# Layer 1's attention with the values as PE's weights: two query tiles move at once, and the root of the mean square is taken on summed columns

## The chip, the core and the metric

The kernel runs on one core of one Trainium2 chip. Time is device time in microseconds (us) from one launch to its end. The engines are PE (matmuls, with weight loads counted apart as PEld), DVE (vector), ACT (activation functions and copies), POOL (GpSimd) and SP, whose queue issues nearly all transfers.

## What is computed

A two-layer block over 512 latent tokens and 256 context tokens of width 1024. Layer 0 is grouped attention in two kinds, layer 1 differential attention; each is followed by a SwiGLU feed-forward. The change lies in layer 1's attention, which has 8 heads of two 64-wide halves:

```python
s = einsum('bqhad,bkhad->bhaqk', qb, k) * scale     # a: the two halves
p = softmax(s, axis=-1)
a = p[:, :, 0] - lam * p[:, :, 1]
o = einsum('bhqk,bkhe->bqhe', a, v)                 # e: 128 values a head
...
o = _rms(o, subln_w) * (1.0 - lam_init)             # over the 128 values of a head
out = o.reshape(n, heads * 128) @ w_out
x = x + gate * out
```

`_rms(x, w)` is x / sqrt(mean(x^2) + EPS) * w. Layer 1 is the last, so only the 512 latent tokens are queries; keys and values come from all 768.

## The kernel before

Tokens are cut into tiles of 128: t = 0..3 latent (NTX = 4), 4 and 5 context (NT = 6 in all). PE's instructions run in the order in which the program writes them; the other engines' and SP's are put in order by a planner that simulates the schedule. Each engine then works its list in order.

Layer 1's attention is a loop over i = 4 h + t (head h, query tile t), 32 steps. `attend1` is a generator with three parts, and the loop runs the parts of different steps beside each other, with two half tiles of the next head's input projection (`step()`, lines 466 to 468) between them:

- `scores(i)`: the two halves' scores on PE (L715, L716), the maximum on DVE (L718), the exponential with its row sum `sm` on ACT (L720), and the combination E0 + rt E1 on DVE (L723 to L727), where rt = -lam sm0 / sm1.
- `transposed(i)`: six PE transposes of the combined 128 x 768 tile (L734), copied to `PT` by ACT (four of them, L739) and DVE (two, L737), so that keys lie on partitions.
- `values(i)`: six fp32 matmuls (L744) with a 128 x 128 piece of `PT` as weights and a 128 x 128 piece of the values `vv` moving, summed in `av`. The output has queries on partitions. ACT scales it by 1 / sm0 (L746) and squares it with a sum along the row (L749); POOL takes (ss / 128 + EPS)^-0.5 (`rsqrt`, L159 and L160); DVE multiplies by root and `subln` (L751) into `o_t[t]`, a 128 x 1024 tile for each query tile.

The output projection needs heads and values on partitions. `OutProj.operand` transposes `o_t[t]` in groups of up to four 128 x 128 pieces on PE (L798), and ACT and DVE write the high part (L799) and the low part (L800) of the result. `term(t, n, k)` then is three matmuls of 512 columns (L807 to L809) for tile t, output half n and head k; `added` empties the bank by a DVE product with the gate (L473) and adds to the residual (L474).

The last six steps, i = 26 to 31 (`last` = 27), and the projection's terms beside them are written out by hand behind the loop, together with the loads and splits of the output weights (`wo1`, L759 and L762). There the order on PE is that of the calls. Two PSUM banks called acc0 and acc1 take the sums: acc0 the projections, acc1 `av` and half of the output sums; two further pairs of banks (`sc`) take scores, and tr0 and tr1 the transposes.

Of the kernel before, what the change touches and what calls it, by code (L numbers as in the profile page):

```python
# [19 lines left out]
P = 128  # L20
# [43 lines left out]
def backbone(es: ExitStack, tc: tile.TileContext, x, c, ctx, c_ctx, mod_w, mod_b, norm_mix_w, norm_ffn_w,  # L64
# [51 lines left out]
    def f32(ap):  # L116
        return ap.bitcast(F32)
# [38 lines left out]
    def rsqrt(ss, n, inv, tag):  # L156

        r = small.tile([P, n], F32, name="rs_" + tag, tag="rs_" + tag)
        nc.gpsimd.tensor_scalar(r, ss, inv, EPS, ALU.mult, ALU.add)  # L159
        nc.gpsimd.tensor_tensor(r, r, neghalf[:, :n], ALU.pow)  # L160
        return r
# [212 lines left out]
    def load_x(t, back=False):  # L374
        xt = keep.tile([P, D], F32, name=f"x{t}", tag="xo", bufs=6)
        src, t0 = (out if back else x, t) if t < NTX else (ctx, t - NTX)
        nc.sync.dma_start(xt, src[0, t0 * P:(t0 + 1) * P, :])
        return xt
# [324 lines left out]
                nc.scalar.copy(kT[:, :, t * P:(t + 1) * P], f32(pk))  # L703
            return transposes

    def attend1(h, t, state, o_t, nlam, subln, mp):
        qs, kT, vv = state.qs, state.kT, state.vv
        mx = small.tile([P, 2], F32, name="mx", tag="mx")
        sm = small.tile([P, 2], F32, name="sm", tag="sm")
        E = []  # L710
        for a in range(2):
            sc = p_sc.pool.tile([P, 1024], F32, name="sc", tag="sc", bufs=2)
            for s0, k0, k1 in ((256, SEQ, TOK), (512, 0, SEQ)):
                so = sc[:, s0:s0 + k1 - k0]
                nc.tensor.matmul(so, qs[t][:, 0, a, :], kT[:, a, k0:k1], start=True, stop=False)  # L715
                nc.tensor.matmul(so, qs[t][:, 1, a, :], kT[:, a, k0:k1], start=False, stop=True)  # L716
            s = sc[:, 256:256 + TOK]
            nc.vector.tensor_reduce(mx[:, a:a + 1], s, AX.X, ALU.max, negate=True)  # L718
# [3 lines left out]
        rc = small.tile([P, 2], F32, name="rc", tag="rc")  # L722
        nc.vector.reciprocal(rc, sm)  # L723

        rt = small.tile([P, 1], F32, name="rt", tag="rt")
        nc.vector.scalar_tensor_tensor(rt, sm[:, 0:1], nlam, rc[:, 1:2], ALU.mult, ALU.mult)
        nc.vector.scalar_tensor_tensor(E[0], E[1], rt, E[0], ALU.mult, ALU.add)  # L727
        yield
        vt = [4, 5, 0, 1, 2, 3]
        pts = []  # L730
        for g0, m in ((0, 4), (4, 2)):
            pt = tr_tile("ppt", [P, 4, P])
            for a in range(m):
                nc.tensor.transpose(pt[:, a, :], E[0][:, (g0 + a) * P:(g0 + a + 1) * P], ident)  # L734
            PT = mp.tile([P, 4, P], F32, name="PT", tag="PT", bufs=3)
            if g0:
                nc.vector.tensor_copy(PT[:, :m], pt[:, :m])  # L737
            else:
                nc.scalar.copy(PT, pt)  # L739
            pts += [PT[:, a, :] for a in range(m)]  # L740
        yield
        av = acc_tile("av", P, one=1)
        for kc, PT in enumerate(pts):
            nc.tensor.matmul(av, PT, vv[:, vt[kc], :], start=kc == 0, stop=kc == NT - 1)  # L744
        oc = o_t[t][:, h * P:(h + 1) * P]
        nc.scalar.activation(oc, av, AF.Copy, scale=rc[:, 0:1])  # L746
        ss = small.tile([P, 1], F32, name="oss", tag="oss")
        o1 = mp.tile([P, P], F32, name="o1", tag="o1", bufs=2)
        nc.scalar.activation(o1, oc, AF.Square, accum_out=ss)  # L749
        r = rsqrt(ss, 1, 1.0 / P, "o")  # L750
        nc.vector.scalar_tensor_tensor(oc, oc, r, subln, ALU.mult, ALU.mult)  # L751


    def out_load(k, raw):
        turn["load"] = nc.sync.dma_start(raw, od_w_out[0, k * P:(k + 1) * P, :])
# [22 lines left out]
    class OutProj:  # L778
# [5 lines left out]
            for i in range(2 if self.l == 0 else 1):  # L784
                self.g[i] = gate_row(self.l, 2, i, pool)

        def operand(self, t, parts=((0, 4), (4, 8)), bank=tr_tile):
            ohi, olo = tile_T(0, t), tile_T(1, t)
            if self.l == 0:
                if self.xs[t] is None:  # L790
                    self.xs[t] = load_x(t)
                nc.scalar.copy(ohi, self.o_t[t])
                nc.vector.tensor_sub(olo, self.o_t[t], f32(ohi))
                return
            for k0, k1 in parts:
                pt = bank("opt", [P, 4, P])
                for k in range(k0, k1):
                    nc.tensor.transpose(pt[:, k - k0, :], self.o_t[t][:, k * P:(k + 1) * P], ident)  # L798
                turn["opt"] = nc.scalar.copy(ohi[:, k0:k1], pt[:, :k1 - k0])  # L799
                nc.vector.tensor_sub(olo[:, k0:k1], pt[:, :k1 - k0], f32(ohi[:, k0:k1]))  # L800
            if k1 == KT:
                self.xs[t] = load_x(t, True)

        def term(self, t, n, k, ps):
            hi, lo = tile_T(0, t)[:, k, :], tile_T(1, t)[:, k, :]
# [760 lines left out]
    if True:  # L1566
# [28 lines left out]
                turned()  # L1595
        nlam = neg_lambda(lqk, cp)
        with behind("load"):
            subln = at.pool.tile([P, P], F32, name="subln")
            nc.sync.dma_start(subln, dram_rows(od_subln[0]))
# [3 lines left out]
        o_t = [keep.tile([P, D], F32, name=f"o{t}", tag="xo", bufs=6) for t in range(NTX)]  # L1603
        xs = xs1
        attend = {}

        def scores(i):
            h, t = divmod(i, NTX)
            attend[i] = attend1(h, t, state[h], o_t, nlam, subln, at.pool)
            next(attend[i])  # L1610

        def transposed(i):
            next(attend[i])

        def values(i):
            if i in attend:
                for _ in attend.pop(i):
                    pass

        last = 8 * NTX - 5  # L1620
        ws, raws = [], []
# [31 lines left out]

        def acc1(name, shape):
            return acc_tile(name, one=1).rearrange("p (k c) -> p k c", c=P)

        def part(*ks):
            if ks[0] == 0:
                part.ps = acc_tile("ops", one=0)
# [2 lines left out]
            if ks[-1] == KT - 1:  # L1662
                oproj.added(0, 0, part.ps, opa.pool, nc.gpsimd)

        def acc1(name, shape):
            return acc_tile(name, one=1).rearrange("p (k c) -> p k c", c=P)
# [52 lines left out]
        values(last + 3)  # L1719
        part(7)  # L1720
        for k in range(4, 6):
            oproj.term(0, 1, k, two[:, 0])
        oproj.operand(1)
        for k in range(6, KT):
# [4 lines left out]
        values(last + 4)  # L1729
        oproj.operand(2)  # L1730
        states[0].close()
        at.close()
# [155 lines left out]
```

## Time and profile before

| | us |
|---|---|
| median of 3 runs | 1695.99 (1693.12 to 1697.33) |
| the profiled execution | 1692.5 |
| its span, first to last instruction | 1690.7 |
| PE busy | 1628.1 (96%) |
| DVE / ACT / POOL busy | 1143.5 / 938.4 / 695.1 |

A row of the profile's groups gives line, engine, operation, the tiles (out<-in), the shape and the count; a row of the timeline gives start, duration, engine, line and shape, and in brackets the idle time before it with what ended it. Durations of matmuls overlap, since they are pipelined: what one costs is the distance from one start to the next.

### The profile page before, as it was taken

How to read it: one execution, taken by the hardware profiler on the slowest of the kernel's cores; microseconds unless marked ns; L12 is line 12 of the kernel's file. 1: busy time of each engine (PE TensorE's matmuls, PEld its weight loads, DVE VectorE, ACT ScalarE, POOL GpSimd, SP SyncE). 2: the span in 40 equal slices, each digit the busy share in tenths (PEclk: the TensorE clock that was granted, in tenths of full speed). 3: DMA queues.
4: the chain of work that ended last, by engine and by line, in shares of the span. 5: the costliest groups of instructions: out<-in, count | busy, mean ns of one | idle time of the engine just before them, and what ended most of it. 6: DMA issues, size and time to landing. Idle time of an engine off the chain costs nothing. (4 is left out here: it accounts for less than half of the span.)

```text
span 1690.7 us, 28553 instructions
## 1 busy us (share of the span) xinstructions
PE 1628.1 (96%) x10378; PEld 1465.3 (87%) x10378; DVE 1143.5 (68%) x2012; ACT 938.4 (56%) x2011; POOL 695.1 (41%) x867
## 2 busy tenths in 40 slices
PE   6999999899999999999999989999999999999998
PEld 3877777677999999998877889999988899999887
DVE  3765656754799887767767656666666598887433
ACT  5565555745456665544664456666666555555321
POOL 2665554321445554412413366666665242221000
PEclk9999999999999999999999999999999999999999
DMA  9222221411455555439966311111112433331431
GB/s 315 75 71 71 73 70 51 173 52 39 134 162 174 165 158 161 135 107 348 307 184 184 98 42 38 47 45 43 46 47 101 124 94 103 108 103 57 137 99 63
DMA packets 217964, 194.64 MB, mean 115 GB/s; under 512 B 20000, under 2 KB 202592, under 8 KB 217824
## 3 DMA queue, kind: packets, MB, share of 16 engines
q1 hardware_dynamic: 217472, 192.62, 36.9%
q8 instruction: 81, 1.33, 0.3%
q14 instruction: 59, 0.48, 0.1%
q10 hardware_dynamic: 352, 0.21, 0.0%
HBM read 179.92 MB, written 12.87 MB: 114 GB/s over the span
## 5 line engine op out<-in xcount | busy, mean ns | idle before, releaser
L901 ACT CAST wbh<-wr 128x512 fp32r<-128x512 f32 x170 | 104.9, 621 | 139.4 <-PE p L933 78.6
L933 PE MATMUL p<-hT,wbh 128*128 128x256 f32 (+1 forms) x752 | 154.4, 299 | 0.0
L911 POOL TENSOR_TENSOR wbl<-wr,wbh 128x512 fp32r<-128x512 f32 x43 | 60.2, 1400 | 174.2 <-ACT wbh L901 174.2
L933 PEld LDWEIGHTS p<-hT,wbh 128*128 128x128 f32 x752 | 121.9, 191 | 0.2
L911 DVE TENSOR_TENSOR wbl<-wr,wbh 128x512 fp32r<-128x512 f32 x127 | 106.4, 847 | 22.2 <-ACT wbh L901 17.8
L933 PE MATMUL p<-hT,wbl 128*128 128x256 f32 (+1 forms) x376 | 111.9, 298 | 0.0
L933 PE MATMUL p<-t,wbh 128*128 128x384 f32 (+1 forms) x480 | 111.3, 318 | 0.0
L604 POOL TENSOR_SCALAR Pt<-Pt,rc 128x256 f32<-128x256 f32 (+3 forms) x96 | 73.1, 772 | 86.9 <-DVE rc L601 79.6
L231 POOL TENSOR_TENSOR modp<-modp 128x512 f32<-128x512 f32 x40 | 57.3, 1433 | 116.5 <-ACT modp L230 116.5
L933 PE MATMUL p<-hTt,wbh 128*128 128x256 f32 (+1 forms) x480 | 101.0, 303 | 0.0
L466 PE MATMUL inps<-wih,hT 128*128 128x384 f32 x256 | 90.0, 351 | 7.2 <-ACT qkv L677 7.2
L887 POOL TENSOR_TENSOR wr<-wr 128x512 f32<-128x512 f32 x40 | 61.6, 1541 | 84.3 <-DVE ws L892 81.9
L933 PE MATMUL p<-b,wbh 128*128 128x384 f32 x368 | 93.8, 336 | 0.4 <-DVE c L961 0.4
L901 ACT CAST wbh<-ws 128x512 fp32r<-128x512 f32 x120 | 69.3, 579 | 42.1 <-PE p L933 31.0
L224 DVE SCALAR_TENSOR_TENSOR ma<-modw,cols,ma 128x256 f32<-128x256 f32 x140 | 87.0, 621 | 2.3
L592 ACT ACTIVATE Pt<-sc,nm 128x256 f32<-128x256 f32 (+3 forms) x96 | 67.8, 708 | 34.8 <-DVE nm L588 18.8
L468 PE MATMUL inps<-wih,hT 128*128 128x384 f32 x256 | 86.1, 336 | 0.0
L467 PE MATMUL inps<-wil,hT 128*128 128x384 f32 x256 | 86.0, 336 | 0.0
L911 DVE TENSOR_TENSOR wbl<-ws,wbh 128x512 fp32r<-128x512 f32 x120 | 81.8, 681 | 2.1 <-ACT wbh L901 2.0
L933 PEld LDWEIGHTS p<-t,wbh 128*128 128x128 f32 x480 | 82.9, 189 | 0.0
L933 PEld LDWEIGHTS p<-hTt,wbh 128*128 128x128 f32 x480 | 78.3, 191 | 3.1 <-ACT modp L230 2.1
L230 ACT ACTIVATE modp<-modw,cols 128x256 f32<-128x256 f32 x160 | 68.3, 499 | 17.1 <-POOL ma L236 8.6
(355 smaller groups left out, 5357.4 us busy)
## 6 DMA issues: line engine op xcount, KB each, us to landing
modw<-in_mod_w_dram SPq DMA_DIRECT2D x96, 512.0 KB, 4.4
wr<-in_ffn_w_in_dram SPq DMA_DIRECT2D x176, 256.0 KB, 3.1
wdr<-in_ffn_w_out_dram SPq DMA_DIRECT2D x66, 512.0 KB, 3.7
wir<-in_od_w_in_dram SPq DMA_DIRECT2D x96, 128.0 KB, 2.3
hidm<-hid SPq DMA_DIRECT2D x44, 192.0 KB, 1.9
hr<-hidm SPq DMA_DIRECT2D x22, 192.0 KB, 3.1
x<-in_x_dram SPq DMA_DIRECT2D x8, 512.0 KB, 6.2
wir<-in_ev_w_in_dram SPq DMA_DIRECT2D x16, 256.0 KB
```

The lines of the kernel that those rows point to most:

```text
L224: nc.vector.scalar_tensor_tensor(acc, w[:, k], scale[k], acc, ALU.mult, ALU.add)
L230: nc.scalar.activation(pr[:, k], w[:, k], AF.Copy, scale=scale[k])
L231: nc.gpsimd.tensor_add(pr[:, 0:2], pr[:, 0:2], pr[:, 2:4])
L466: nc.tensor.matmul(ps, hs[0][:, k, :], a, start=k == 0, stop=False)
L467: nc.tensor.matmul(ps, hs[0][:, k, :], b, start=False, stop=False)
L468: nc.tensor.matmul(ps, hs[1][:, k, :], a, start=False, stop=k == KT - 1)
L592: turn["exp"] = nc.scalar.activation(p[:, :n], s, AF.Exp, bias=nm[:, c1], accum_out=sm[:, c1])
L604: nc.gpsimd.tensor_scalar(p[:, :n], p[:, :n], rc[:, hh:hh + 1], 1.0, ALU.mult, ALU.mult)
L887: nc.gpsimd.tensor_sub(w, raw[f, "G1"], w)
L901: nc.scalar.copy(hi, w)
L911: (nc.gpsimd if name == "G2" else nc.vector).tensor_sub(lo, raw[need[n]], f32(hi))
L933: nc.tensor.matmul(ps, w[:, k, :], H[b][h][:, k, :], start=first and k == 0 and q == 0, stop=final and k == 3 and q == 2, skip_group_check ...
```

## The change

The value product is turned round: a 128 x 128 piece of `vv` is the weights and the transposed scores of two query tiles (t even and t + 1, together 256 columns) move, so there are six matmuls for a pair of tiles, and the output has the head's 128 values on partitions and queries along the row. That is the layout which the output projection wants, so `operand` copies without a transpose and `o_t[t]` is 128 x (8 x 128).

The sum of squares now runs over partitions. ACT writes the squares and, apart, the product scaled by `subln` (now one number a partition). For each tile of the pair a matmul with the squares as weights and a column of ones moving gives the sums with queries on partitions; DVE adds EPS sm0^2 in place of a division by sm0, POOL takes the power, for both tiles at once. The roots have to be spread over partitions again: for heads 0 to 6 they are written to memory and read back to all partitions, by two transfers on SP's queue; for head 7 DVE multiplies the identity by the roots and one matmul of ones with it gives the spread rows in PSUM. DVE multiplies by them. `PT` is one tile for a pair, with one buffer, in place of three of four pieces each.

`attend1` has two more parts: `values(i)` and `squares(i)` do something for odd i only, `scaled(i)` finishes. In the loop squares(i - 2) and scaled(i - 3) come behind scores(i); at the end they are placed by hand, and the sums of the output tile (1,1) take bank acc0 (`part2`) instead of acc1.

```diff
-    def attend1(h, t, state, o_t, nlam, subln, mp):
+    def attend1(h, t, state, o_t, nlam, subln, mp, pair):
...
+        if t % 2 == 0:
+            pair["PT"] = mp.tile([P, NT, 2, P], F32, name="PT", tag="PT")
+        PT = pair["PT"]
         for g0, m in ((0, 4), (4, 2)):
             pt = tr_tile("ppt", [P, 4, P])
             for a in range(m):
                 nc.tensor.transpose(pt[:, a, :], E[0][:, (g0 + a) * P:(g0 + a + 1) * P], ident)
-            PT = mp.tile([P, 4, P], F32, name="PT", tag="PT", bufs=3)
...
+            (nc.vector.tensor_copy if g0 else nc.scalar.copy)(PT[:, g0:g0 + m, t % 2, :], pt[:, :m])
         yield
-        av = acc_tile("av", P, one=1)
-        for kc, PT in enumerate(pts):
-            nc.tensor.matmul(av, PT, vv[:, vt[kc], :], start=kc == 0, stop=kc == NT - 1)
-        oc = o_t[t][:, h * P:(h + 1) * P]
-        nc.scalar.activation(oc, av, AF.Copy, scale=rc[:, 0:1])
-        ss = small.tile([P, 1], F32, name="oss", tag="oss")
-        o1 = mp.tile([P, P], F32, name="o1", tag="o1", bufs=2)
-        nc.scalar.activation(o1, oc, AF.Square, accum_out=ss)
-        r = rsqrt(ss, 1, 1.0 / P, "o")
-        nc.vector.scalar_tensor_tensor(oc, oc, r, subln, ALU.mult, ALU.mult)
-
+        if t % 2 == 0:
+            return
+        vt = [4, 5, 0, 1, 2, 3]
+        av = acc_tile("av", one=1)
+        for kc in range(NT):
+            nc.tensor.matmul(av[:, 0:2 * P], vv[:, vt[kc], :], PT[:, kc].rearrange("p a q -> p (a q)"),
+                             start=kc == 0, stop=kc == NT - 1)
+        o1 = mp.tile([P, 2, P], F32, name="o1", tag="o1")
+        nc.scalar.activation(o1.rearrange("p a q -> p (a q)"), av[:, 0:2 * P], AF.Square)
+        om = mp.tile([P, 2, P], F32, name="om", tag="om", bufs=2)
+        nc.scalar.activation(om.rearrange("p a q -> p (a q)"), av[:, 0:2 * P], AF.Copy, scale=subln)
+        yield
+        for a in range(2):
+            nc.tensor.matmul(av[:, 2 * P + a:2 * P + a + 1], o1[:, a, :], cst[:, C_ONE:C_ONE + 1], start=True, stop=True)
+        r = small.tile([P, 2], F32, name="rs_o", tag="rs_o")
+        ss = small.tile([P, 2], F32, name="oss", tag="oss")
+        nc.vector.scalar_tensor_tensor(ss, psm[:, 0, :], EPS, psm[:, 0, :], ALU.mult, ALU.mult)
+        nc.vector.scalar_tensor_tensor(r, av[:, 2 * P:2 * P + 2], 1.0 / P, ss, ALU.mult, ALU.add)
+        nc.gpsimd.tensor_tensor(r, r, neghalf[:, :2], ALU.pow)
+        if h < 7:
+            mem = dram.tile([2, P], F32, name="rmem", tag="rmem", bufs=4)
+            nc.sync.dma_start(mem.rearrange("a q -> q a"), r)
+            rq = mp.tile([P, 2, P], F32, name="rq", tag="rq", bufs=2)
+            nc.sync.dma_start(rq.rearrange("p a q -> p (a q)"), dram_rows(mem.rearrange("a q -> (a q)")))
+            yield
+        else:
+            yield
+            for a in range(2):
+                nc.vector.tensor_scalar(o1[:, a, :], ident, r[:, a:a + 1], None, ALU.mult)
+            rb = acc_tile("rb", one=1)
+            nc.tensor.matmul(rb[:, 0:2 * P], cst[:, C_ONE:C_ONE + P], o1.rearrange("p a q -> p (a q)"), start=True, stop=True)
+            rq = rb[:, 0:2 * P].rearrange("p (a q) -> p a q", a=2)
+        for a in range(2):
+            nc.vector.tensor_tensor(o_t[t - 1 + a][:, h, :], om[:, a, :], rq[:, a, :], ALU.mult)
...
             for k0, k1 in parts:
-                pt = bank("opt", [P, 4, P])
-                for k in range(k0, k1):
-                    nc.tensor.transpose(pt[:, k - k0, :], self.o_t[t][:, k * P:(k + 1) * P], ident)
-                turn["opt"] = nc.scalar.copy(ohi[:, k0:k1], pt[:, :k1 - k0])
-                nc.vector.tensor_sub(olo[:, k0:k1], pt[:, :k1 - k0], f32(ohi[:, k0:k1]))
...
+                nc.scalar.copy(ohi[:, k0:k1], self.o_t[t][:, k0:k1])
+                nc.vector.tensor_sub(olo[:, k0:k1], self.o_t[t][:, k0:k1], f32(ohi[:, k0:k1]))
...
         for i in range(last - 1):
             scores(i)
+            squares(i - 2)
+            scaled(i - 3)
...
         scores(last - 1)
-        oproj.operand(0, ((0, 4),), acc1)
+        scaled(last - 4)
+        oproj.operand(0, ((0, 4),))
         transposed(last - 2)
         part(0)
...
         wo1()
+        squares(last - 2)
         scores(last)
         transposed(last - 1)
         part(1, 2)
-        values(last - 1)
         wo1()
+        scaled(last - 2)
         scores(last + 1)
-        oproj.operand(0, ((4, 7),), acc1)
+        oproj.operand(0, ((4, 7),))
...
         scores(last + 2)
+        squares(last)
         transposed(last + 1)
         part(4)
-        values(last + 1)
+        scaled(last)
...
         part(5)
+        values(last + 2)
         wo1()
-        values(last + 2)
+        squares(last + 2)
         scores(last + 4)
         part(6)
-        oproj.operand(0, ((7, 8),), acc1)
+        scaled(last + 2)
+        oproj.operand(0, ((7, 8),))
+        oproj.operand(1)
...
         transposed(last + 4)
-        oproj.sums(1, 0, opa.pool, nc.gpsimd, range(1))
+        ops = acc_tile("ops", one=0)
+        for k in range(4):
+            oproj.term(1, 0, k, ops)
         values(last + 4)
+        for k in range(4, KT):
+            oproj.term(1, 0, k, ops)
+        squares(last + 4)
+        oproj.added(1, 0, ops, opa.pool, nc.gpsimd)
+        part2 = acc_tile("ops", one=0)
+        for k in range(3):
+            oproj.term(1, 1, k, part2)
+        scaled(last + 4)
         oproj.operand(2)
...
-        oproj.sums(1, 1, opa.pool, nc.gpsimd, range(1, 2))
+        for k in range(3, KT):
+            oproj.term(1, 1, k, part2)
+        oproj.added(1, 1, part2, opa.pool, nc.gpsimd)
         oproj.operand(3)
         oproj.sums(2, 0, ns=range(1))
```

More of the change, by code (lines that the diff above doesn't have):

```diff
@@ L704, in finish @@
             return transposes
-    def attend1(h, t, state, o_t, nlam, subln, mp):
+    def attend1(h, t, state, o_t, nlam, subln, mp, pair):
         qs, kT, vv = state.qs, state.kT, state.vv
         mx = small.tile([P, 2], F32, name="mx", tag="mx")
-        sm = small.tile([P, 2], F32, name="sm", tag="sm")
+        if t % 2 == 0:
+            pair["sm"] = small.tile([P, 2, 2], F32, name="sm", tag="sm")
+        psm = pair["sm"]
+        sm = psm[:, :, t % 2]
         E = []
@@ L785, in gates, with operand @@
                 self.g[i] = gate_row(self.l, 2, i, pool)
[L787 removed]
+        def operand(self, t, parts=((0, 8),)):
             ohi, olo = tile_T(0, t), tile_T(1, t)
[L789 to L794, printed above, removed]
[L795 to L802 removed]
+            for k0, k1 in parts:
+                nc.scalar.copy(ohi[:, k0:k1], self.o_t[t][:, k0:k1])
+                nc.vector.tensor_sub(olo[:, k0:k1], self.o_t[t][:, k0:k1], f32(ohi[:, k0:k1]))
+            if k1 == KT and self.xs[t] is None:
+                self.xs[t] = load_x(t, self.l == 1)
         def term(self, t, n, k, ps):
@@ L1597, in backbone @@
         with behind("load"):
-            subln = at.pool.tile([P, P], F32, name="subln")
-            nc.sync.dma_start(subln, dram_rows(od_subln[0]))
+            subln = at.pool.tile([P, 1], F32, name="subln")
+            nc.sync.dma_start(subln, od_subln.rearrange("o d -> d o"))
             nc.gpsimd.tensor_scalar(subln, subln, 1.0 - LAM_INIT, 1.0, ALU.mult, ALU.mult)
@@ L1602, in backbone @@
         gate_mem(1, 5, 0)
-        o_t = [keep.tile([P, D], F32, name=f"o{t}", tag="xo", bufs=6) for t in range(NTX)]
+        o_t = [keep.tile([P, KT, P], F32, name=f"o{t}", tag="xo", bufs=6) for t in range(NTX)]
         xs = xs1
-        attend = {}
+        attend, pair = {}, {}
         def scores(i):
             h, t = divmod(i, NTX)
-            attend[i] = attend1(h, t, state[h], o_t, nlam, subln, at.pool)
+            attend[i] = attend1(h, t, state[h], o_t, nlam, subln, at.pool, pair)
             next(attend[i])
@@ L1615, in values, with squares, scaled @@
         def values(i):
-            if i in attend:
-                for _ in attend.pop(i):
-                    pass
+            if i % 2 and i in attend:
+                next(attend[i])
+        def squares(i):
+            if i % 2 and i in attend:
+                next(attend[i])
+        def scaled(i):
+            for _ in attend.pop(i, ()):
+                pass
         last = 8 * NTX - 5
@@ L1718, in backbone @@
             oproj.term(0, 1, k, two[:, 0])
-        values(last + 3)
         part(7)
[L1721 to L1724, printed above, removed]
+        for k in range(4, KT):
             oproj.term(0, 1, k, two[:, 0])
```

19 lines of the change are left out of this document (5 added, 14 removed).

## The prediction

> **What bounds the kernel now.** First the page's engine table, then the table by stretches for the stage that the change touches (layer 1's attention, about 1000 to 1345 us), then who PE waited for in it.
>
> ```profile
> PE 1628.1 (96%) x10378; PEld 1465.3 (87%) x10378; DVE 1143.5 (68%) x2012; ACT 938.4 (56%) x2011; POOL 695.1 (41%) x867
> ...
> 1000.00:1250.00 250.00, 244.27 (x1712) 235.05 (x1711) 160.08 (x328) 162.08 (x422) 165.31 (x265) 1.00 0.15 41
> 1250.00:1295.00 45.00, 39.26 (x262) 33.99 (x261) 34.12 (x64) 34.35 (x81) 27.82 (x42) 1.00 0.30 104
> 1295.00:1345.00 50.00, 49.41 (x273) 42.13 (x273) 23.96 (x42) 24.98 (x51) 14.90 (x20) 1.00 0.28 86
> ...
> PE inps L466 <- ACT qkv L677: 3.8, 7, 0.6
> ...
> PE ops L809 <- DVE hT L800: 1.4, 1, 1.4
> ...
> PE av L744 <- DVE PT L737: 0.9, 1, 0.9
> PE qpt L696 <- ACT qt L698: 0.8, 1, 0.8
> PE ppt L734 <- DVE e L727: 0.8, 1, 0.8
> PE av L744 <- ACT PT L739: 0.6, 1, 0.6
> ```
>
> The columns of a stretch are its length and the busy time of PE, weight loads, DVE, ACT and POOL. In the head loop (first row) PE is busy 244 of 250 us, the other engines about 160; the first wait row is its largest, 3.8 us in seven waits. In the hand-written end of the stage (second row) PE stands 5.7 us of 45, and the other wait rows (1250 to 1300; a row is who waited for whom, the sum, how often, the longest) say for whom. So PE's order and length set the time. An engine that gets faster can give back at most those 5.7 + 5.7 us; an instruction more on PE is paid in full.
>
> **The change part by part.** *The value products.* Each fp32 matmul leaves two records (192 in the code, 384 in the trace).
>
> ```profile
> L744 PE MATMUL av<-vv,PT x384: 270/275/378, 1014.9 to 1307.9; 128*128 128x128 f32 x192
> L623 PE MATMUL av<-Pt,vv x400: 379/379/431, 93.8 to 394.0; 128*64 128x256 f32 x134
> 1014.87 1.50 PE L744 MATMUL av<-vv,PT 128*128 128x128 f32 x12
> 1267.77 0.94 PE L744 MATMUL av<-vv,PT 128*128 128x128 f32 x7
> 93.83 1.08 PE L623 MATMUL av<-Pt,vv 128*64 128x256 f32 x8
> 393.70 0.65 PE L623 MATMUL av<-Pt,vv 128*64 128x256 f32 x4 [0.19 <-DVE Pt L615]
> ```
>
> Now: five records more make 0.56 us, 0.112 each, so a pair of tiles costs 24 x 0.112 = 2.69. After: 12 records with 256 moving columns. Layer 0 has that shape at half width, in two halves that write different partitions: four records more take 0.43. If the halves run side by side, a record costs 0.215; one after the other, 0.108. I take 0.215, because a record of 256 columns also lasts 104 ns longer than one of 128 (379 against 275), which put on 0.112 gives 0.216. A pair is then 2.58, 0.11 less, over 16 pairs -1.8 us. The other end, 0.108, would be -22 us; it is a rival below.
>
> The Trainium skill's page "TensorE: Matmul & The Clock Gate", section "Back-to-back issue gap", speaks for that end: in a stream of load and matmul it gives about 81 ns for 128 columns and 131 ns for 512, far from four times as much. By its 131 for what two passes of 256 columns amount to, a pair would take 1.57, or -18 us in all. The trace does not bear it out: 512 columns cost 0.24 a matmul, as the rows of the output projection below show, so width is paid in proportion.
>
> *The squares' sums.* New on PE: two matmuls a pair with the squares as weights and one moving column, 4 records. The nearest rows are four such records with four columns, in a stream:
>
> ```profile
> 517.20 0.50 PE L252 MATMUL modcol<-cst,ma 128*128 128x4 f32 x4
> 517.56 0.59 PE L933 MATMUL p<-hT,wbh 128*128 128x384 f32 x2
> 518.16 0.51 PE L933 MATMUL p<-hT,wbh 128*128 128x384 f32 x2
> ```
>
> 0.36 to the next start, and what follows takes 0.08 longer than usual: 0.44 a pair, +7.0 us over 16. Fewer columns will hardly make it less, since a record with four (0.44 / 4 = 0.11) already costs what one with 128 does: the weights are the price.
>
> *The output transposes* go: 32 of L798.
>
> ```profile
> 1298.24 1.03 PE L798 MATMUL opt<-cst,o 128*128 128x128 f32 x8
> 1299.03 0.48 PE L807 MATMUL ops<-wo,hT 128*128 128x512 f32 x1
> 1299.34 0.40 PE L808 MATMUL ops<-wo,hT 128*128 128x512 f32 x1
> 1299.58 0.39 PE L809 MATMUL ops<-wo,hT 128*128 128x512 f32 x1
> ```
>
> Eight take 0.79, and the next step 0.31 in place of 0.24: 0.108 each, -3.4 us. The last head's two broadcasts (2 records of 256 columns, about 0.07 around them) add 2 x 0.5 = +1.0. PE's work: -1.8 + 7.0 - 3.4 + 1.0 = **+2.8 us**.
>
> *New and lost waits on PE, at the end of the stage*, where its order is written by hand:
>
> ```profile
> 1264.87 0.51 PE L809 MATMUL ops<-wo,hT 128*128 128x512 f32 x1 [1.37 <-DVE hT L800]
> ...
> 1272.00 1.57 PE L744 MATMUL av<-vv,PT 128*128 128x128 f32 x12
> ...
> 1273.63 0.39 ACT L746 ACTIVATE o<-av,rc 128x128 f32<-128x128 f32 x1
> 1274.05 0.31 ACT L749 ACTIVATE o<-o 128x128 f32<-128x128 f32 x1
> 1261.22 0.44 ACT L420 ACTIVATE sq<-qkv 128x256 f32<-128x256 f32 x1
> 1277.95 1.06 ACT L759 CAST wo<-wor 128x1024 fp32r<-128x1024 f32 x1
> ...
> 1320.58 0.39 PE L809 MATMUL ops<-wo,hT 128*128 128x512 f32 x1
> 1321.01 0.70 DVE L473 TENSOR_TENSOR ops<-ops,g 128x512 f32<-128x512 f32 x1 [4.06 <-PE ops L809]
> ...
> 1277.59 0.56 POOL L160 TENSOR_TENSOR rs_o<-rs_o,neghalf 128x1 f32<-128x1 f32 x1
> 1288.94 0.35 DVE L751 SCALAR_TENSOR_TENSOR o<-o,rs_o,subln 128x128 f32<-128x128 f32 x1 [0.23 <-POOL rs_o L160]
> 1289.21 0.21 DVE L726 SCALAR_TENSOR_TENSOR rt<-sm,nlam,rc 128x1 f32<-128x1 f32 x1
> ```
>
> Lost: the first product of the output projection waits 1.37 for an operand that hung on a transpose; now it is copied from finished heads, early. -1.4.
>
> squares(25) and squares(29) stand right behind their value products in PE's order. The last value record starts at 1272.00 + 11 x 0.112 = 1273.23, ACT begins 0.40 later. It then has a square and a scaled copy of 256 columns (0.44 each by L420; the sums go into the same bank, so I let PE wait for both) and the hand-back: 1.3 after the last start, where 0.2 would be usual. 1.1 us each if ACT is free, 0.6 if only the square is waited for, 2.1 behind a cast like L759. I take 1.5 each: +3.0. squares(27) has a tile's scores in front (four matmuls of 512 columns and four of 256, at 0.24 and half of it 1.4 us), squares(31) four terms (twelve of 512, 2.9), so nothing.
>
> rb(29) and rb(31): from the last sum to the broadcast lie 0.4, a small DVE step (0.21, as L726), the power (0.56), two DVE products with the identity (0.35 each, as L751) and three hand-overs that I put at 0.1: 2.2 us. Over it lie a tile's scores and a term (1.4 + 0.7), and three terms (2.1). It just fits; with another DVE step of the size of L473 in front 0.8 is lost. I take 0.5 + 0.3 = +0.8, with 0 and 1.6 as ends.
>
> The bank acc0 is now used three times running: (1,0), the new part2 and (2,0); before, (1,1) lay in acc1. DVE empties it 0.43 + 0.70 after the last start, 1.2 with the hand-over, in place of 0.24. Between the first two lie squares(31), 0.44; between the second nothing. 0.55 + 1.0 = +1.55.
>
> *Off PE.* ACT drops two scalings and two squares a pair (2 x 0.7 us, and the reads of their sums) for two steps of 256 columns (0.9). DVE trades two scalings for two products and two small steps, about even; POOL loses one power of two. The operand's copies keep their size, PT's too. ACT's half microsecond and more a pair can give back part of the loop's waits for qkv; I take -1.0, ends 0 and -3.8.
>
> *The broadcast through memory* (heads 0 to 6, 14 pairs): two transfers on SP's queue, the second waiting for the first, with weight loads behind both; DVE's products wait for the second, and the score maxima and PT copies are queued behind them.
>
> ```profile
> hidm<-hid SPq DMA_DIRECT2D x44, 192.0 KB, 1.9
> hr<-hidm SPq DMA_DIRECT2D x22, 192.0 KB, 3.1
> lqk<-in_od_lq_dram SPq DMA_DIRECT2D x2, 0.2 KB, 5.1
> L718 DVE TENSOR_REDUCE mx<-sc x64: 939/950/959, 1001.7 to 1292.3; 128x1 f32<-128x768 f32 x64
> SPq L365 <- POOL rs_q L159: 161.8, 7, 29.1
> ```
>
> A write and a read back take 1.9 + 3.1 = 5.0 us by the median of another tensor, the power and its queue 1 to 2. From squares to scaled is one turn of the loop, (1292.3 - 1001.7) / 31 = 9.4 us. So I cost it at nothing; that cover goes if a transfer of 4-byte pieces takes 5.1 like lqk's (a rival).
>
> Sum: 2.8 - 1.4 + 3.0 + 0.8 + 1.55 - 1.0 = +5.8 us. The profiled execution took 1692.5 us (span 1690.7 and 1.8 around it), so 1698.3 for it; it lay 3.5 under the median of the runs, 1695.99, on which the forecast is put: **1701.8**. About 0.3%, 5.1 us, is what a measurement can tell from no change, so the sum is just outside.
>
> **The rivals.** *The covers hold:* ACT serves the squares at once, DVE the roots. Then 2.8 - 1.4 + 1.2 + 0 + 1.1 - 2.5 = +1.2, or 1697.2. For it: ACT is idle a quarter of the end. Against: 34.35 of 45 us busy is an average over a stage in which exponentials come in pairs.
>
> *ACT's relief clears the waits (faster).* Place: loop and end; price: -3.8 for the loop's waits on qkv, -3.1 for the four on PT, qt and e at the end, -1.4 for the first term's, against +2.8 of work, and no new stall: -5.5, or 1690.5. It decides if the ACT time saved lies right before the copies of qkv that PE waits for. Against: those seven waits are short, at most 0.6, and follow each time on a bank that has just been filled, which a lighter ACT does not change.
>
> *The transfers come late (slower still).* At 5.1 each the chain is 5.1 + 5.1 + 1.5 = 11.7 us against 9.4, so 2.3 late a pair, and DVE stands at the product. SP itself has stood up to 29.1 us at a weight load (last row), and a root queued behind one would be late too. DVE is busy 160 of 250 us, so its slack takes most; a third may reach PE, 14 x 2.3 / 3 = 10.7, with the forecast's own terms +16.5, 1712.5. Against: DVE's L751 waits for its root already, and no row of PE's waits names it.
>
> *The wide products are cheap:* 0.108 a record, 1701.8 - 22 + 1.8, or about 1682.
>
> **How the numbers follow.** Forecast 0.55 (own range +2 to +10 us; 0.36 of it over 5.1, 0.19 under), covers hold 0.15, transfers late 0.17, relief 0.10, cheap products 0.03. Slower 0.36 + 0.17 = 0.53, within 0.3% 0.34, faster 0.13. The range 1691 to 1714 leaves out the cheap products, most of the relief and the upper half of the late transfers, together under 0.2 of the chance.
>
> **What would show it.** In the new profile: 192 records of the value products at about 0.215, not 0.11; 64 records of the sums at 0.11; no L798; PE waiting for ACT ahead of the sums of pairs 25 and 29 by 1 to 2 us, and for the emptying of acc0 (L473) ahead of part2 and (2,0); no wait of 1.4 at the first output term. DVE waiting for the transfer by over 1 us a pair, with PE waiting for PT behind it, would show the late transfers. Value records at 0.11, or a loop whose idle time on PE falls from 5.7 to under 2 us, would make the forecast wrong on the fast side.

## The result, and the profile after

The changed kernel takes **1836.24 us** (median of 4, 1833.1 to 1838.0) beside 1695.61 for the kernel before (4 runs, 1693.12 to 1697.33) on the same chip: a ratio of 1.0824, interval 1.081 to 1.0837. That is 141 us more where the forecast said 6. The profiled execution has a span of 1831.3 us.

First the stage again, from the first score to the last term of the output projection: by the table by stretches, for the kernel before, the one after, and a later experiment (e6_both, below) whose PE list is that of the kernel after. Behind the busy times stand PE's granted clock, the busy share of the transfer engines and GB/s.

```profile
999.20:1340.90 341.70, 329.64 (x2213) 307.78 (x2214) 216.54 (x430) 219.69 (x547) 207.29 (x324) 1.00 0.18 55
```
```profile
1000.10:1481.40 481.30, 371.35 (x2057) 330.24 (x2058) 215.15 (x463) 208.67 (x480) 191.12 (x277) 0.88 0.16 43
```
```profile
1001.70:1370.00 368.30, 339.78 (x2057) 308.77 (x2058) 225.80 (x463) 210.17 (x480) 193.87 (x277) 0.98 0.23 56
```

The stage went from 341.7 to 481.3 us, so it holds 139.6 of the 141. Two parts: PE stood 12.1 us and now stands 110.0, and its busy time went from 329.6 to 371.4. Most of the second is not more work: the same 2057 records take 339.8 in e6_both, 31.6 less, where the granted clock is 0.98 and not 0.88; some 10 us are the change's own work. PE stands, and then runs slower. For whom it stands, by the waits of PE, DVE and ACT in the stage:

```profile
PE av L746 <- ACT PT L739: 37.0, 6, 6.5
PE inps L466 <- ACT wih L370: 27.6, 5, 5.8
PE ppt L738 <- DVE rc L726: 12.2, 1, 12.2
PE inps L467 <- POOL wil L371: 7.3, 6, 1.3
...
DVE o L774 <- DMA rq<-rmem: 146.8, 14, 10.9
...
ACT e L723 <- DVE mx L721: 84.5, 29, 8.8
```

and by the transfers (issues, KB each, median us from issue to landing):

```profile
rmem<-rs_o SPq DMA_DIRECT2D x14, 1.0 KB, 8.6
```

The write of 1 KB takes 8.6 us to land, where the forecast had 1.9 from another tensor. DVE stands at each of the 14 products, 10.5 us on average, and what is queued behind it there is what the forecast named: the score maxima. One turn, followed through the timeline:

```profile
1032.96 0.37 SPq L762 DMA_DIRECT2D rmem<-rs_o  x1
1041.57 0.34 SPq L764 DMA_DIRECT2D rq<-rmem  x1
...
1035.09 0.28 DVE L422 TENSOR_REDUCE qss<-sq 128x2 f32<-128x128 f32 x1
1046.22 0.49 DVE L774 TENSOR_TENSOR o<-om,rq 128x128 f32<-128x128 f32 x2 [10.85 <-DMA rq<-rmem]
1047.30 0.95 DVE L721 TENSOR_REDUCE mx<-sc 128x1 f32<-128x768 f32 x1
...
1048.29 0.90 ACT L723 ACTIVATE e<-sc,mx 128x768 f32<-128x768 f32 x1 [8.76 <-DVE mx L721]
...
1051.33 5.17 PE L746 MATMUL av<-PT,vv 128*128 128x256 f32 x12 [6.50 <-ACT PT L739]
1056.15 0.47 PE L702 MATMUL kpt<-identr,kd 128*128 128x128 f32 x2
```

DVE had work up to 1035.4 and then stood for the product; the maxima came at 1047.3, the exponential after 8.76 us of waiting, the copies of PT behind it, and PE stood 6.50. The last two rows show the second loss: the 12 value records take 1056.15 - 1051.33 = 4.82 us, 0.40 each. The first row below gives the granted clock of that stretch, 0.51 (third figure from the end). Where PE had not stood before them (e7_mended, below), the same 12 take 2.40, at a clock of 1.00:

```profile
1051.33:1056.15 4.82, 4.82 (x13) 3.90 (x13) 3.00 (x6) 1.25 (x4) 3.04 (x5) 0.51 0.00 0
...
1044.27 2.75 PE L746 MATMUL av<-PT,vv 128*128 128x256 f32 x12
1046.67 0.48 PE L702 MATMUL kpt<-identr,kd 128*128 128x128 f32 x2
```

This is what the Trainium skill's page "TensorE: Matmul & The Clock Gate", section "HAM oscillation — how this bites in real kernels", warns of: PE idle for more than about 3.4 us falls back to half its clock. The trace agrees with the factor of two, 0.40 against 0.20 us a record and a clock of 0.51 against 1.00 behind a stand of 6.5 us; it does not fix the threshold.

The second chain is on SP. The read back stands at the head of SP's list until the write has landed, and the weight loads of the next head (`wir`, split on ACT and POOL into `wih` and `wil`) are behind it. SP stands there 112.3 us in 14 waits. (It stands 156.1 for the roots themselves, ahead of the writes; but in e7c, below, the version nearest to the kernel before, that is still 127.4, so it is not what costs.)

```profile
1062.20 0.36 SPq L762 DMA_DIRECT2D rmem<-rs_o  x1
1070.64 0.33 SPq L764 DMA_DIRECT2D rq<-rmem  x1
1071.09 14.59 SPq L365 DMA_DIRECT2D wir<-in_od_w_in_dram  x12
...
1077.49 0.83 ACT L370 CAST wih<-wir 128x768 fp32r<-128x768 f32 x1 [7.66 <-DMA wir<-in_od_w_in_dram]
...
1078.37 0.58 PE L466 MATMUL inps<-wih,hTc 128*128 128x256 f32 x1 [5.41 <-ACT wih L370]
```

### The profile page after: what moved, and what is told of

Its sections match the earlier page's. It is cut to its first block, busy times and chain, and to the rows that moved or that the text cites. A ratio compares the mean times of both kernels' runs of the same rounds, so it can differ in the third digit from the quotient of the medians.

```text
span 1831.3 us, 28211 instructions
## 1 busy us (share of the span) xinstructions
PE 1671.7 (91%) x10222; PEld 1487.7 (81%) x10222; DVE 1146.8 (63%) x2045; ACT 927.1 (51%) x1944; POOL 678.6 (37%) x819
## 5 line engine op out<-in xcount | busy, mean ns | idle before, releaser
L946 PE MATMUL p<-hT,wbl 128*128 128x256 f32 (+1 forms) x376 | 111.9, 298 | 0.0
L746 PE MATMUL av<-PT,vv 128*128 128x256 f32 x192 | 68.6, 528 | 43.5 <-ACT PT L739 37.0
L723 ACT ACTIVATE e<-sc,mx 128x768 f32<-128x768 f32 x64 | 57.5, 901 | 85.1 <-DVE mx L721 84.5
L774 DVE TENSOR_TENSOR o<-om,rq 128x128 f32<-128x128 f32 x28 | 7.0, 289 | 146.8 <-DMA rq<-rmem 146.8
L746 PEld LDWEIGHTS av<-PT,vv 128*128 128x128 f32 x192 | 51.9, 279 | 56.4 <-ACT PT L739 38.9
```

The costliest lines, as they stand in the source:

```text
L746: nc.tensor.matmul(av[:, 0:2 * P], vv[:, vt[kc], :], PT[:, kc].rearrange("p a q -> p (a q)"), start=kc == 0, stop=kc == NT - 1)
L946: nc.tensor.matmul(ps, w[:, k, :], H[b][h][:, k, :], start=first and k == 0 and q == 0, stop=final and k == 3 and q == 2, skip_group_check ...
```

## The experiments

Theories: **A**, DVE stands at the product, and the maxima behind it make PE stand; **B**, SP stands at the read, and the weight loads behind it come late; **C**, the long write costs by itself, by making other transfers late; **D**, PE's new instructions cost more than counted. All four can hold; the runs are to give each its size.

**e1_matmul_spread: no transfers.**
```diff
-        if h < 7:
+        if h < 0:
```


> The changed kernel with head 7's way of spreading the roots (identity times roots, one matmul of ones) used for all eight heads, so that no root goes through memory. Theory A (DVE stands 10.5 us a pair at the product that waits for the transfers, and PE's exponentials and copies behind it) and rival B (SP's queue stands at the read back, and the weight loads behind it come late): both 1705 to 1715, that is the forecast's terms and 14 x 0.5 us more on PE. Rival C (the turned products, their sums or PE's lower clock cost the time): still over 1800.

Measured: 1714.65 (1710.9 to 1716.82), ratio 1.0112 (1.0096 to 1.0127). PE's waits in the stage, and the groups of the two kinds of new matmuls:

```profile
PE inps L467 <- POOL wil L371: 3.5, 6, 0.8
PE inps L466 <- ACT qkv L677: 2.7, 4, 0.9
...
PE av L754 <- ACT om L751: 1.7, 2, 0.9
```
```profile
L771 PE MATMUL rb<-o,cst 128*128 128x256 f32 x32 | 9.7, 386 | 1.3 <-DVE o L769 1.2
L754 PE MATMUL av<-cst,o 128*128 128x1 f32 x64 | 8.2, 232 | 1.7 <-ACT om L751 1.7
```

Every large wait is gone, and 122 of the 141 us with them: they belong to the way through memory. Of the 19 us that stay, 18.2 are in the stage (359.9 us for 341.7): 13.2 more of PE's work, which includes 14 more spreads, and 5.0 more of standing. They are for D, below.

**e2_two_turns: the product two turns later, tied behind that turn's score maxima on DVE (A).**
```diff
-            scaled(i - 3)
+            scaled(i - 5)
...
+        with behind(*(["mx"] if h < 7 else [])):
```


> The changed kernel with the same transfers, but in the loop the product with the roots is called two turns later and tied behind the score maxima of that turn, so that DVE has other work while the transfers run. Theory A: the twelve pairs of the loop lose their 10.5 us, the two pairs at the end keep part of theirs: 1705 to 1730, and DVE's waits at the product fall from 147 to under 25 us. Rival B: SP still stands 8.5 us a pair ahead of the weight loads, so PE's waits for the split weights (about 35 us) stay: 1740 to 1760. Rival C: no change, 1836.

Measured: 1778.74 (1777.32 to 1782.45), 57.5 us less than the kernel after. Its waits:

```profile
PE inps L466 <- ACT wih L370: 27.9, 5, 6.1
PE ppt L738 <- DVE rc L726: 12.3, 1, 12.3
PE inps L467 <- POOL wil L371: 7.3, 6, 1.3
```

The 37.0 us for ACT's PT are gone, so A is shown, at 57.5 us with the clock's share. The time lies above what I had expected from either theory (at most 1730 by A, 1760 by B). The waits for weights (27.9 and 7.3, before 27.6 and 7.3) have not moved, and a long one for DVE remains: it lies in the hand-written end, where head 6's products still come soon after their roots.

**e3_eight_bytes: the same 1 KB, written as 128 pieces of 8 bytes in place of 256 of 4.**
```diff
-            mem = dram.tile([2, P], F32, ...)
-            nc.sync.dma_start(mem.rearrange("a q -> q a"), r)
+            mem = dram.tile([P, 2], F32, ...)
+            nc.sync.dma_start(mem, r)
```


> The changed kernel with the two roots of a query side by side in memory: 128 pieces of 8 bytes are written in place of 256 of 4; the read back is the same size. If the write is paid by the piece, it falls from 8.5 to about 4.3 us, DVE's stand by 4 us a pair, and the time to about 1780. If it is a fixed price of a small write, it stays at 1836. Theory A needs the time to follow the length of the write about one to one; rival C expects no change.

Measured: 1724.63 (1724.21 to 1725.44), 111.6 less than after. The write lands in about a third of the time, and the stands at the product fall by more than half:

```profile
rmem<-rs_o SPq DMA_DIRECT2D x14, 1.0 KB, 3.0
```
```profile
L775 DVE TENSOR_TENSOR o<-om,rq 128x128 f32<-128x128 f32 x28 | 7.1, 296 | 60.8 <-DMA rq<-rmem 60.8
```

I had expected half the pieces to take half the write's time, and the kernel to come down to 1780; it came down twice as far. DVE still stands 60.8 us (4.3 a pair), yet of PE's long waits only one of 8.5 is left, in the end: what DVE's slack covers is about 4 us a pair, and not 10.5.

**e4_write_probe: what makes the write long.** e1, with a write of another form in each of heads 0 to 6 and a read behind it on SP, for which nothing that computes waits.

```diff
+        if h < 7:
...
+            if h == 0:
+                mem = dram.tile([2, P], F32, name="pa", tag="pa", bufs=2)
+                nc.sync.dma_start(mem.rearrange("a q -> q a"), r)
+                nc.sync.dma_start(got.rearrange("p a q -> p (a q)"), dram_rows(mem.rearrange("a q -> (a q)")))
...
+            elif h == 2:
+                mem = dram.tile([2, P, P], F32, name="pc", tag="pc", bufs=2)
+                nc.sync.dma_start(mem[:, :, 0].rearrange("a q -> q a"), r)
+                nc.sync.dma_start(got[:, 0, 0:2], mem[:, :, 0].rearrange("a q -> q a"))
...
-        if h < 7:
+        if h < 0:
```


> Kernel e1 (nothing waits for the probes) with a write and a dependent read of a different form in each of heads 0 to 6, to read the length of each: 256 pieces of 4 bytes packed (as in the changed kernel), 128 of 8 bytes packed, 256 of 4 bytes each 512 bytes apart, 128 of 4 bytes packed, one row of 1 KB, 128 rows of 512 bytes, 128 pieces of 64 bytes. Paid by the piece: 8.5, 4.3, 8.5, 4.3, 2, 4, 4. Paid for pieces that fall into the same stretch of memory: 8.5, 8, 2 to 3, 5, 2, 2, 4 or more. A fixed price of any small write: all about 8.5 except the rows. Time of the kernel as e1 within 1%.

Measured: 1730.55, one run. SP's timeline; the read starts when its write has landed, so the difference of two rows is the write. pa: 256 pieces of 4 bytes, packed; pb: 128 of 8 bytes, packed; pc: 256 of 4 bytes, each 512 bytes from the next; pd: 128 of 4 bytes, packed; pe: one row of 1 KB.

```profile
1031.77 0.37 SPq L766 DMA_DIRECT2D pa<-rs_o  x1
1040.88 0.34 SPq L767 DMA_DIRECT2D got<-pa  x1
...
1081.49 0.34 SPq L770 DMA_DIRECT2D pb<-rs_o  x1
1084.94 0.34 SPq L771 DMA_DIRECT2D got<-pb  x1
...
1123.04 0.37 SPq L774 DMA_DIRECT2D pc<-rs_o  x1
1124.65 0.37 SPq L775 DMA_DIRECT2D got<-pc  x1
...
1164.55 0.34 SPq L778 DMA_DIRECT2D pd<-rs_o  x1
1172.06 0.34 SPq L779 DMA_DIRECT2D got<-pd  x1
...
1210.15 0.25 SPq L782 DMA_DIRECT2D pe<-om  x1
1211.27 0.34 SPq L783 DMA_DIRECT2D got<-pe  x1
```

9.1, 3.4, 1.6, 7.5 and 1.1 us. (Two more forms, 128 rows of 512 bytes and 128 pieces of 64, took 1.4 to 3.5, longer with other loads in front.) The number of pieces is not the price: 256 spread apart are the fastest of the small ones, and half as many packed are nearly as slow as all. It is small pieces side by side in one stretch of memory: counted by pieces to 512 bytes, 128 take 9.1 and 7.5 us (pa, pd), 64 take 3.4 (pb), one takes 1.6 (pc). The Trainium skill's page "DMA: Bandwidth & Descriptors", section "Specifications", says that a transfer under 512 bytes is done as read, change and write back; pieces that share a stretch would then have to follow each other. The rows are as that would have it, but they also show that small pieces by themselves cost little (pc), which the sentence alone does not tell. Besides, PE waited 11.3 us in three waits for `wih` here, though DVE never stood for a transfer: B or C, without A.

**e5_read_later: the read later, on SP (B).** e2, with the read in a step of its own, two turns behind the write.
```diff
             nc.sync.dma_start(mem.rearrange("a q -> q a"), r)
+            if h < 6:
+                yield
...
+            with behind("mx"):
+                nc.sync.dma_start(rq.rearrange("p a q -> p (a q)"), dram_rows(mem.rearrange("a q -> (a q)")))
...
+            if i < 26:
+                squares(i - 4)
             scaled(i - 5)
```


> Like e2 (products two turns of the loop after the write), but for heads 0 to 5 the read back is issued on SP two turns after the write, one turn ahead of its product, so that SP does not stand between the two and the weight loads pass. The write stays as long as it is (8.3 to 8.8 us). Theory B (what e2 left, 83 us above the kernel before, comes mostly from weight loads that stand on SP's queue behind a read that waits for its write): PE's waits for wih and wil, 27.9 and 7.3 us in e2, fall to about the 3.5 us of e1, ACT's 40.3 us for wir to under 10; with the throttle's share about 35 to 40 us less, 1738 to 1745, and what stays is the hand-written end (head 6's roots, 12 us of PE waiting for DVE there) and the work of PE. Theory A (DVE alone: the length of the write reaches PE only through DVE's order): nothing changes, 1775 to 1782.

Measured: 1779.86 (1778.62 to 1781.11), e2 again; but SP's timeline shows that nothing was tested:

```profile
1053.37 0.36 SPq L762 DMA_DIRECT2D rmem<-rs_o  x1
1061.75 0.33 SPq L767 DMA_DIRECT2D rq<-rmem  x1
1062.19 14.89 SPq L365 DMA_DIRECT2D wir<-in_od_w_in_dram  x12
```

The planner sorts SP's list itself, and the tie, to an instruction of DVE, does not bind it: the read stood where it had stood. A place in the program is no place in a queue.

**e6b_read_on_act: the same on ACT's queue, behind the exponentials.**
```diff
+            with behind("exp"):
+                (nc.scalar if h < 6 else nc.sync).dma_start(rq..., dram_rows(mem...))
```


> What e5 wanted to do, and did not: there the read back stayed on SP's list right behind its write, ahead of the weight loads. Here it is e5 with the reads of heads 0 to 5 on ACT's queue, behind the exponentials of the turn before the product, some 18 us after the write is issued, so nobody stands for the write of 8.6 us, and SP's list holds only writes and weight loads. Theory B (weight loads that stand behind a read which waits for its write): ACT's 40 us of waits for wir and PE's 28.8 for wih go, PE's 7.3 for wil falls to about 5; with the throttle's share 35 to 45 us less than e2's 1778.7, so 1735 to 1745. What stays is head 6 at the end (about 25 us of PE's waits for DVE, and its share of the throttle). Theory A (DVE's order alone): 1775 to 1782.

Measured: 1761.05 (1760.77 to 1762.4), 17.7 less than e2, half of what I had expected from B. Waits for weights, SP's rows and the weight loads' median landing:

```profile
PE inps L466 <- ACT wih L370: 8.1, 5, 2.0
```
```profile
1056.70 0.37 SPq L762 DMA_DIRECT2D rmem<-rs_o  x1
1061.90 15.27 SPq L365 DMA_DIRECT2D wir<-in_od_w_in_dram  x12
```
```profile
wir<-in_od_w_in_dram SPq DMA_DIRECT2D x63, 128.0 KB, 4.0
```

SP's stand at the reads fell from 111.9 us in e2 to 15.0, and the wait for `wih` from 27.9 to 8.1, so B is shown. It does not go to nothing, though no load stands behind a read: the loads of a head now start 5 us after a write, while it is under way, and the stage's 63 land in 4.0 us by the median, 2.3 in e1. That speaks for C. It is not the only delay: in the kernel after, the six loads issued right behind a read, when the write has already landed, take 5.3 us by the median (1055 to 1080 us), and the six behind those 2.2. How much of B is standing and how much this, the runs do not part. The gain is also net of a new stand, of ACT, which the next pair shows.

**e7b_mended_four_bytes and e7c_eight_on_act: the end mended, then the write alone (C).** e7b is e6b with heads 6 and 7 by the matmul, the two squares' sums behind the next scores, and `part2` in a free bank; e7c is e7b with pieces of 8 bytes and no other difference.
```diff
-        if h < 7:
+        if h < 6:
...
-        squares(last - 2)
         scores(last)
+        squares(last - 2)
...
-        squares(last + 2)
         scores(last + 4)
+        squares(last + 2)
...
-        part2 = acc_tile("ops", one=0)
+        part2 = two[:, 1]
```


> The run before plus e7's edits at the end (heads 6 and 7 by the matmul, the free bank, the two squares' sums later), with the pieces of 4 bytes and their write of 8.6 us left as they are. If the length of the write costs only through who stands behind it, all of the 141 us go but what e7 kept: 1703 to 1712, the same as e7 with its short write. If the write costs by itself (by holding transfer engines that the weight loads need), 5 to 20 us more than e7.

> e7b with pieces of 8 bytes: nothing else differs (e7, the earlier one of that kind, also had its read on SP). Theory C (the long write costs by itself, since weight loads that are issued while it is under way land later: 3.8 us by the median in e7b, 2.4 in e7): loads land in about 2.4 us again, PE's waits for wih (8.2) vanish and the time is e7's, 1704 to 1710. Rival (the read on ACT's queue is what costs e7b its 26 us over e7): it stays at 1728 to 1736 with wih's waits.

Measured: e7b 1733.49 (1732.55 to 1736.56), e7c 1706.16 (1701.56 to 1707.68; ratio 1.0042, 1.0027 to 1.0056). The landing of the loads and the write, of e7b and then of e7c:

```profile
wir<-in_od_w_in_dram SPq DMA_DIRECT2D x63, 128.0 KB, 3.8
...
rmem<-rs_o SPq DMA_DIRECT2D x12, 1.0 KB, 8.4
```
```profile
wir<-in_od_w_in_dram SPq DMA_DIRECT2D x63, 128.0 KB, 2.4
...
rmem<-rs_o SPq DMA_DIRECT2D x12, 1.0 KB, 3.7
```

PE's waits for `wih`, 8.2 us in e7b, are gone in e7c, and those for `wil` fell from 8.2 to 3.6. The form of the 1 KB write is worth 27.3 us. Not all of it is C: at the last of the twelve reads ACT itself stood until the write had landed, in e7b for 8.13 us (the row below), in e7c for 2.15, and a wait of 4.5 of PE for ACT's copy of `qt` follows in e7b alone.

```profile
1288.55 0.42 ACT L420 ACTIVATE sq<-qkv 128x256 f32<-128x256 f32 x1 [8.13 <-DMA rmem<-rs_o]
```

That stand begins behind the last write. From the first write to the last e7b takes 246.05 us (1032.39 to 1278.44) and e7c 222.45 (1035.98 to 1258.43), and in that time nothing stood for a write: 23.6 us are left for C. So C is shown, and in size it is near B. e7b lies 25.7 us above e7 (below), where I had expected 5 to 20. The records of the transfers do not show the write holding the transfer engines: the 272 packets of the one issued at 1032.39, which lands after 8.7 us, all lie between 1033.2 and 1033.6. What happens until it lands they do not tell.

**e6_both, e7_mended, e8_mended_r, e11_best: how low it goes.** e6_both is e2 and e3 together; e7_mended adds e7b's end to it (read on SP); e8 sums the squares in fp32r, in which a matmul leaves one record in place of two; e11 is e8 with the read on ACT's queue. The edit of e8 (`oner` is two columns of ones in fp32r):
```diff
-        o1 = mp.tile([P, 2, P], F32, name="o1", tag="o1")
+        o1 = mp.tile([P, 2, P], F32R, name="o1", tag="o1")
...
-            nc.tensor.matmul(av[:, 2 * P + a:2 * P + a + 1], o1[:, a, :], cst[:, C_ONE:C_ONE + 1], start=True, stop=True)
+            nc.tensor.matmul(av[:, 2 * P + 2 * a:2 * P + 2 * a + 2], o1[:, a, :], oner, start=True, stop=True)
```

> The edits of e2 and e3 together: pieces of 8 bytes (write about 3 us in place of 8.6) and the product two turns later. Both theories: DVE's stands at the product (60.8 us in e3) go in the loop; in e3 they reached PE only as 8.5 us at the end, where head 6's products are not moved, so at most a few us less than e3's 1724.6: 1712 to 1722. If it is e3 again within 2 us, DVE's slack had taken all stands of 4 us a pair already; if it falls below 1705, they cost PE more than its named waits show.

> e6 with four more edits at the end: heads 6 and 7 spread their roots by the matmul, the sums of output tile (1,1) take a free bank in place of acc0, and the two squares' sums that stood right behind their value products come behind the next scores. Gone by that: 8.5 us of waits for DVE's small steps behind head 6's products, 1.6 for acc0's emptying, 1.7 for the squares; two more spreads on PE at 0.5 = +1.0. From 1717 that is about 1706; by the forecast's own terms without waits it is 1696 + 2.8 + 1.0 - 1.4 = 1698. So 1698 to 1707. Above 1712 there is a cost that neither the waits nor the count of PE's work names.

> e7 with the squares rounded to fp32r and summed so (two columns of ones moving, each column the same sum), so that a tile's sum is one pass in place of two: 32 records of the sums in place of 64. If the weights are the price (as the forecast said of the sums: four records 0.36 us, and 0.08 on what follows), a pair goes from 0.44 to about 0.22 and the whole gains 3.5 us: 1695 to 1703, near or below the kernel before. If a record's latency in the pipeline is the price and not the count, under 1 us.

> e8 (pieces of 8 bytes, products two turns later, heads 6 and 7 by the matmul, sums in fp32r) with the read on ACT's queue. e8 kept 5.5 us of PE waiting for the low half of the weights; if that comes from reads standing 2.8 us on SP it goes, and 1704 to 1707 results; PE's work in the stage, 334.6 us against 329.6 before, keeps it above the kernel before. At or below 1696 it would be the version to take.

Measured: e6_both 1721.65 (1719.45 to 1724.39), e7 1707.81 (ratio 1.0072, 1.0059 to 1.0085), e8 1710.45 (1.0081, 1.0065 to 1.0098), e11 1707.42 (1.0062, 1.005 to 1.0074). e6_both is 3 under e3, so DVE's slack had indeed taken nearly all stands of 4 us. e7 came out just above the range I had given (1698 to 1707), and so did e11 (1704 to 1707): its read on ACT's queue left 5.2 us of waits for `wil`, where e8 had 5.5. e8 was expected at 1695 to 1703. In it a pair's sums cost 0.14 where they cost 0.36, as hoped, by the timeline:

```profile
1034.17 0.28 PE L756 MATMUL av<-oner,o 128*128 128x2 f32 x2
1034.31 0.36 PE L468 MATMUL inps<-wih,hTc 128*128 128x256 f32 x1
```

That is 3.5 us of work, and the time did not fall, which I had not expected. In the stage PE's busy time fell by 2.3 (336.9 to 334.6) and the stage by 0.5 (355.2 to 354.7): most of it came back as waits. That e8 measured longer than e7 lies ahead of the stage, which its profiled execution reached 3.8 us later (1003.5 for 999.7). No version comes down to the kernel before; the nearest, e7c, is 0.3 to 0.6% above it.

## Why the prediction was wrong

*The account.* On one path, in the order of the runs: DVE's order 57.5 (after to e2), SP's order 17.7 (to e6b), the hand-written end 27.6 (to e7b, four edits at once), the long write 27.3 (to e7c), and 8.9 between e7c and the kernel before run beside it (1697.25). That is 139 of the 141 us; another order of the steps would share them otherwise, since e3 took 111.6 at one stroke by shortening the write: A, B and C all hang on its length.

*The step that failed* is "The broadcast through memory", costed at nothing because "From squares to scaled is one turn of the loop", 9.4 us, which was to cover the transfers. Three things were wrong in it. The write was priced by the median of a tensor with wide rows (1.9 us) and took 8.6, the read about 4.6: 13.3 from issue to product. The row with pieces of 4 bytes, lqk's 5.1, stood beside it and was nearer in kind; even that was too low. Next, the cover: one turn of the program was counted, but DVE's list had only 2.4 us of work between the root (issued at 1032.96) and the stand, because the planner put the product in front of the next turn's maxima. And the price of a stand on PE was taken as the stand alone; PE also ran the next records at half speed (clock 0.51). The weight loads behind the transfers were named ("with weight loads behind both") and not priced.

*The rivals.* "The transfers come late" was the right mechanism at an eighth of its size (16.5 us in all, where 141 were measured): it had 2.3 us late a pair, of which a third reaches PE; it was 10.5 late a pair. DVE's slack took about 4 of them, as e3 shows, and the rest could reach PE. "Wide products cheap": value records stand 0.20 apart, not 0.108, so the row of layer 0 was read rightly; by the Trainium skill's page "TensorE: Matmul & The Clock Gate", section "Back-to-back issue gap", an estimate would have put them nearer 0.13.

*The other terms.* The sums' stretch (0.36 to the next start), acc0's two waits (1.6 for 1.55) and the lost wait at the first output term came as forecast; the squares' waits were 1.7 for 3.0, and the waits for `qkv`, 5.2 in the whole stage before, are 2.7 in e1's, more than the 1.0 less that I had credited; but those for `wil` rose from 1.0 to 3.5 and took it back. PE's work was too small: in e1 the stage holds 342.9 us of PE work against 329.6 before, 13.2 more, where the forecast's terms give 2.8 and 14 more spreads at 0.5, together 9.8. Which rows hold the other 3.4 stays open: the busy times of the spreads (9.7 for 16) and the sums (8.2) overlap with what follows, and from start to next start a spread takes 0.24, a pair's sums 0.36 and a pair's value records 2.40 (forecast 2.58). So without any transfer the change was still slower, by 1.1% in e1.

*What stays open:* why packed pieces of 4 bytes are so slow and how they delay other loads; and the 9 us between e7c and the kernel before. In the stage e7c takes 10.2 us more (351.9 for 341.7): 8.0 of PE's work (337.6 for 329.6) and 2.2 of standing in many short waits, not one cause.

## What to carry to other kernels

A transfer's price hangs on its pieces: take it from a row with the same width of piece and the same layout, and if there is none, give it its worst neighbour. Cover is counted in the list of the engine that will stand, from the instruction that the planner puts behind it, and on every queue that a waiting instruction heads. A stand of PE of several microseconds is to be charged twice, once as it is and once for the work behind it, which runs at half speed for a while: here 98 us more of standing came with 32 us of slower records.

## What the runs showed of the hardware

- Writes to memory, from issue to landing, by the medians of the runs and the rows of e4: 256 packed pieces of 4 bytes 8.3 to 9.1 us; 128 of 4 bytes 7.5; 128 of 8 bytes 2.7 to 3.7; 256 of 4 bytes 512 bytes apart 1.6; one row of 1 KB 1.1.
- Where loads are issued on the same queue while such a write is under way (e6b, e7b), the 63 loads of the stage land in 3.8 to 4.0 us by the median in place of 2.3 to 2.4, though none of them waits for the write.
- Behind a stand of 6.5 us twelve fp32 records with 256 columns take 4.82 us, at a granted clock of 0.51, in place of 2.40 at 1.00; over the stage the same 2057 records took 371.4 us at a granted clock of 0.88 and 339.8 at 0.98.
